# Second weight buffers for block 5, values 35 steps behind, and the end's first sums in dead keys' memory, in a one-core hybrid decoder layer

## The chip, the cores and the metric

The kernel runs on one core of a Trainium2 chip. The metric is the device time in microseconds of one execution. All numbers of the profile come from one execution taken by the hardware profiler; the times come from three other executions.

## What is computed

One decoder layer on 1024 tokens of width 1024, in float32. The input is normalized, projected to queries, keys, values and gates, and goes through two mixers side by side: eight heads of differential softmax attention, and four heads of gated linear attention (GLA). Both results are normalized by head, gated, joined, projected by `w_out`, normalized and added to the input. Cut to what the change touches, the reference is:

```python
h = rms_norm(x, pre_g)
z = jnp.einsum('bsd,de->bse', h, w_in)
qa, ka, va, ga, qb, kb, vb, gb, gk_low = split_columns(z)
# per head, two maps m = 0, 1 of width 64, causal:
s = jnp.einsum('bqhmd,bkhmd->bhmqk', qb, k)
p = jax.nn.softmax(jnp.where(mask, s, -jnp.inf), axis=-1)
w = p[:, :, 0] - lam * p[:, :, 1]
oa = jnp.einsum('bhqk,bkhv->bqhv', w, v)
oa = rms_norm(oa, subln_g) * (1.0 - lam_init)
oa = oa.reshape(B, S, DA_WIDTH) * jax.nn.silu(ga)
# ob: the GLA heads, normalized and gated
y = jnp.einsum('bse,ed->bsd', jnp.concatenate([oa, ob], axis=-1), w_out)
out = x + rms_norm(y, post_g)
```

## The kernel before

[...] The kernel has three stages.

**Projections and GLA.** Until about 634 us TensorE multiplies the normalized input by `w_in` with a Strassen-like scheme, and the four GLA heads run between. Queries, keys, values and gates of the attention heads go to DRAM (`q_d`, `k_d`, `v_d`, `g_d`), the GLA half of the mixed activations to `mixe`, and the split `w_out` to `wo_d`. This stage isn't changed.

**Attention.** Three generators yield pieces of work with a cost, and `merge` puts them in one order: it always takes a piece of the stream whose clock stands lowest. The first, `all_scores`, runs over 8 heads and in each over the query blocks 7 to 0 of 128 rows. A block and map gives one or two matmul pairs into a PSUM bank (`sc`, three banks in turn); a score takes the keys (`k`) and the same with the high and low parts swapped (`ks`). DVE moves the bank to `p0` or `p1` with the running minimum (L1037), ACT takes the exponential (L1047), POOL scales map 1 (L1053), and DVE joins both maps (L1056). What results is the weight tile `p0_{qb}`; blocks 6 and 7 have two buffers of it, blocks 0 to 5 one. The second stream, `all_values`, runs 34 units behind: `turn` transposes a weight tile (`wtr`), ACT and DVE split it (L1095, L1096), and `weigh` multiplies by the values (`po`). `attn_norm` then normalizes and gates a half head: two matmuls `ms`, the gate loaded from `g_d` (L1118), a multiplication on POOL (L1140), and a store to `mixd` (L1141). The third stream, `out_early`, multiplies what is ready by `w_out`: the GLA half of all eight row blocks, then heads 0 to 3 (`ypart`, banks `Y`). Its sums go through `yst` (two buffers, L1246) to `y_d`, the second time added by POOL's DMA (L1304).

TensorE's order is just the order in which the program is written, so `merge` decides it. The orders of the other engines and of the DMA queue on SP come from a scheduler, which places an instruction as soon as its inputs and buffers allow in its own timeline.

**The end.** When thirteen of the fourteen stores of heads 0 to 6 have been placed, `mix_pair` loads heads 4 to 6 of two row blocks (`m_raw`, L1210; split in L1331 and L1332). The sums so far are loaded from `y_d` into `yp`, a tile of the same two `yst` buffers (L1312, L1323, L1338), and ACT copies them into a PSUM bank (`seed`, L1365), so that the last matmuls (`yps`) add to them. `ENDS` is the order of the row blocks, 4 5 6 7 0 1 2 3. Then `finish` takes each block through the last norm, with `post_g` loaded in L1392 and negated on POOL in L1394.

Loads of keys and queries: `load_qk` takes one of six tags of the pool `kp` (`q0`, `q1`, `k0`, `k1`, `ks0`, `ks1`: query or key, lower or upper half of the sequence). Odd heads have their lower keys in another pool. The next head's upper half is asked for when block 4 has been placed, as only blocks 7 to 4 read it.

Of the kernel before, what the change touches and what calls it, by code (L numbers as in the profile page):

```python
# [8 lines left out]
F32 = mybir.dt.float32  # L9
# [5 lines left out]
P = 128  # L15
# [16 lines left out]
def hymba_kernel(  # L32
# [23 lines left out]
    def fp(t):  # L56
        return t.bitcast(F32)
# [810 lines left out]
    def load_qk(h, n, half):  # L868

        if h % 2 and half == 0 and n != "q":  # L870
            t = smps[0].tile([P, 2, 512], F32R, tag=f"{n}0", name=f"{n}0")
        else:
            t = kp.tile([P, 2, 512], F32R, tag=f"{n}{half}", name=f"{n}{half}")
        for m in range(2):
            d = qk_d["q" if n == "q" else "k"][h][m, :, :, cols(half)]
            if n != "ks":
                sp.dma_start(fp(t[:, m]), d.rearrange("t p s -> (t p) s"))
            else:
                for i in range(2):
                    sp.dma_start(fp(t[64 * i : 64 * i + 64, m]), d[1 - i])  # L880
        qk[h, n, half] = t

    qk, smps = {}, []


    go(order.index((12, 5)) - made[0])
# [98 lines left out]
    def load_v(h):  # L985
        v = [smp.tile([P, NT, P], F32R, tag="v", name=f"v{t}", bufs=4) for t in range(2)]
        for t in range(2):
            ins = sp.dma_start(fp(v[t]), v_d[h][t])
            if h == 0:
                tc.keep_in_program_order(ins)  # L990
        return v
# [16 lines left out]
    def scores(h, qb):  # L1008

        n = (qb + 1) * P  # L1010
        qc = slice(qb % 4 * P, qb % 4 * P + P)
        st = const.tile([P, 6], F32, tag="stt", name="stt", bufs=4)
        p0 = pp.tile([P, n], F32, tag=f"p0_{qb}", name="p0", bufs=1 + (qb > 5))
        p1 = smp.tile([P, S], F32, tag="p1", name="p1", bufs=2)
        for m, p in enumerate((p0, p1)):
            q = qk[h, "q", qb // 4][:, m, qc]
            parts = parts_of(n)
            if h == DA_HEADS - 1 and (qb, m) in ((1, 1), (0, 0), (0, 1)):

                parts = [(0, 512)]  # L1020
            for i, (a, b) in enumerate(parts):
                sc = sc_bank("sc", [P, 512])
                for j, name in enumerate(("k", "ks")):
                    for half in range(2):
                        lo, hi = max(a, half * 512), min(b, half * 512 + 512)
                        if lo < hi:
                            mm(
                                sc[:, lo - a : hi - a], q,
                                qk[h, name, half][:, m, lo - half * 512 : hi - half * 512],
                                start=(j == 0), stop=(j == 1),  # L1030
                            )
                e = min(b, n)
                last = i == len(parts) - 1

                behind = tc.issue_after(lowest[0]) if (h, qb) == (0, NT - 2) else nullcontext()
                with behind:
                    ins = dve.tensor_tensor_reduce(  # L1037
                        p[:, a:e], sc[:, : e - a],
                        maskt[:, NZ + P - (e - a) :] if last else maskt[:, : e - a],
                        1.0, 3e38 if i == 0 else st[:, 4 + m : 5 + m], ALU.add, ALU.min,  # L1040
                        st[:, m : m + 1] if last else st[:, 4 + m : 5 + m],
                    )
                if (h, qb) == (0, NT - 1):
                    lowest[:] = [ins.ins]
                c = 0.08 + (e - a) / 512 * 0.56
                if last:
                    act.activation(  # L1047
                        p[:, :n], p[:, :n], AF.Exp, bias=st[:, m : m + 1], scale=-1.0,
                        accum_out=st[:, 2 + m : 3 + m],
                    )  # L1050
                if last and m:
                    dve.reciprocal(st[:, 4:6], st[:, 2:4])  # L1052
                    pool.tensor_scalar(  # L1053
                        p1[:, :n], p1[:, :n], st[:, 5:6], lam, ALU.mult, ALU.mult
                    )
                    dve.scalar_tensor_tensor(  # L1056
                        p0[:, :n], p0[:, :n], st[:, 4:5], p1[:, :n], ALU.mult, ALU.subtract
                    )
                    w[h, qb] = p0
                    c += 0.25 + n / 1024 * 1.4  # L1060
                yield c
# [3 lines left out]
    def all_scores():  # L1065
        for h in range(DA_HEADS):
            for qb in range(NT - 1, -1, -1):
                if qb in (3, 5) and h:
                    yield lambda h=h, half=qb // 4: (h - 1, half) in used
                yield from scores(h, qb)  # L1070
                if qb == 4 and h + 1 < DA_HEADS:
                    for n in ("q", "k", "ks"):
                        load_qk(h + 1, n, 1)
                    for n in ("k", "ks"):
                        load_qk(h + 1, n, 0)
            if h + 1 < DA_HEADS:
                load_qk(h + 1, "q", 0)
        scored.append(True)
        opened.update(dict.fromkeys(SC))
# [33 lines left out]
    def attn_norm(h, half, o):  # L1113
        if h < DA_HEADS - 1:
            gate = smp.tile([P, 512], F32, tag="gate", name="gate", bufs=2)
        else:
            gate = kp.tile([P, 512], F32, tag=("q1", "k1")[half], name="gate")
        sp.dma_start(gate, g_d[h][:, cols(half)])  # L1118
        sq = smp.tile([P, 512], F32, tag="r", name="sq", bufs=1)
        act.activation(sq, o, AF.Square)  # L1120
        hl = smp.tile([P, 2, 512], F32R, tag="sq_hl", name="sq_hl", bufs=1)
        act.copy(hl[:, 0], sq)
        dve.tensor_tensor(hl[:, 1], sq, fp(hl[:, 0]), ALU.subtract)
        if h == DA_HEADS - 1:

            dve.scalar_tensor_tensor(gate, o, sub_g, gate, ALU.mult, ALU.mult)
        yield 0.0
        yield 0.0
        n_tr[0] += 1
        ms = bank(TR[n_tr[0] % 2], [P, 512], "ms")  # L1130
        for i in range(2):
            mm(ms, ones, hl[:, i], start=(i == 0), stop=(i == 1))
        if h == DA_HEADS - 1 and not half:
            opened[TR[n_tr[0] % 2]] = None
        r = smp.tile([P, 512], F32, tag="r", name="r", bufs=1)
        act.activation(r, ms, AF.Ln, bias=eps_t, scale=1.0 / P)
        act.activation(r, r, AF.Exp, scale=-0.5)
        if h < DA_HEADS - 1:
            dve.scalar_tensor_tensor(r, o, sub_g, r, ALU.mult, ALU.mult)
            pool.tensor_tensor(gate, r, gate, ALU.mult)  # L1140
            sp.dma_start(mixd[h * P : (h + 1) * P, cols(half)], gate)  # L1141
            stored.append(h)
        else:
            dve.tensor_tensor(gate, gate, r, ALU.mult)
            last_mix[half] = gate
        yield 0.0

    def all_values():
# [17 lines left out]
        for i, (h, half, kts) in enumerate(units):  # L1166
# [10 lines left out]
                yield 0.4  # L1177
                norm_step()
            if kts == (0,):
                o = smp.tile([P, 512], F32, tag="o", name="o", bufs=3)  # L1180
                po = bank(PO, [P, 512], "po")
            weigh(po, half, kts, vs[h], turned[h, half, kts])
            norm_step()
# [65 lines left out]
    def out_early():  # L1249
# [57 lines left out]
        for n, st in enumerate(ENDS[:2]):  # L1307
            if n:
                yield lambda: scored
            for dh in range(2):  # L1310
                yp = smp.tile([P, 512], F32, tag="yst", name="yp", bufs=2)
                sp.dma_start(yp, yd[st][dh])  # L1312
                seed(st, dh, (Y, SC)[n][dh], yp)
            yield 0.7
        for st in ENDS[:2]:
            for dh in range(2):
# [2 lines left out]
                    yield 0.69  # L1319
            if st == ENDS[0]:  # L1320
                mix_pair(2)
                yp = smp.tile([P, 512], F32, tag="yst", name="yp", bufs=2)
                sp.dma_start(yp, yd[ENDS[2]][0])  # L1323
                seed(ENDS[2], 0, SC[2], yp)

    def mix_pair(n):

# [6 lines left out]

    def early_ends():

        yp = smp.tile([P, 512], F32, tag="yst", name="yp", bufs=2)
        sp.dma_start(yp, yd[ENDS[2]][1])  # L1338
        for e in range(4, 7):
            last_times(ENDS[2], 0, parts_d[ENDS[2]], e)  # L1340
        for st in ENDS[:2]:
            last_part(st, parts_d[st])
            for dh in range(2):
                last_times(st, dh, parts_d[st], 7)
        seed(ENDS[2], 1, PO, yp)
        for st in ENDS[2:4]:
            last_part(st, parts_d[st])

# [18 lines left out]
    def last_times(st, dh, part, e):  # L1367
# [6 lines left out]
            )  # L1374

    T = 8 * 36.0
    LAG = 34.0
    s_cost = sum(
        2 * sum(0.08 + (min(b, n) - a) / 512 * 0.56 for a, b in parts_of(n)) + 0.25 + n / 1024 * 1.4
        for n in range(P, S + 1, P)  # L1380
# [1 line left out]
    merge(  # L1382
        [0.0, T, DA_HEADS * s_cost, all_scores()],
        [LAG, T + LAG, DA_HEADS * 10.0, all_values()],
        [-6.0, T + LAG, 16.0 + 14 * 5.52 + 16 * 2.76 + 11.8, out_early()],
    )


    smp_cm.__exit__(None, None, None)
    fin = ctx.enter_context(tc.tile_pool(name="fin", bufs=3, reuse_waits="tile"))  # L1390
    post_g = fin.tile([P, D], F32, name="post_g", bufs=1)
    sp.dma_start(post_g, post_norm_g[0:1, :].to_broadcast([P, D]))  # L1392

    pool.tensor_scalar(post_g, post_g, -1.0, None, ALU.mult)  # L1394
# [118 lines left out]
```

## Time and profile before

| | us |
|---|---|
| three runs: median | 999.5 |
| lowest and highest | 996.18, 999.75 |
| the profiled execution | 1000.02 |
| its span, first to last instruction | 998.3 |
| projections and GLA, to the first `ypart` | 633.9 |
| attention, to the first `yps` | 300.2 |
| from the first `yps` to the last matmul | 56.5 |
| after the last matmul | 7.7 |

The profile names a group by source line, engine, operation and tile. TensorE's matmuls all have line 117 and its transposes line 120, so their tiles tell them apart: `sc` for scores, `wtr` for transposed weights, `po` for values, `ypart` and `yps` for the output projection. A wait is written as the instruction that waits, its line, and what ended the wait; idle time of an engine stands in brackets in the timeline. "SPq" is the DMA queue on SP, and its times are those of issuing, not of the transfer.

### The profile page before, as it was taken

What the parts mean: (1) busy time and instruction counts of PE and PEld (TensorE: products, weight loads), DVE (VectorE), ACT (ScalarE), POOL (GpSimd) and SP (SyncE); (2) the same over time, 40 slices, a digit from 0 to 9 for tenths busy, and PEclk for the clock granted to TensorE, in tenths of its full rate; (3) what the DMA queues carried; (4) which work ended last, traced back from release to release, by engine and by line L of the source; (5) the groups of instructions that cost most, each with busy time, mean ns of one, the idle gap of its engine ahead of it and who ended that gap; (6) DMA issues with size and microseconds to landing.
All of it is one profiled execution on the core that took longest, in us unless ns stands there. A gap on an engine that the chain in (4) does not pass through costs nothing.

```text
span 998.3 us, 15795 instructions
## 1 busy us (share of the span) xinstructions
PE 966.6 (97%) x5354; PEld 835.4 (84%) x5354; DVE 728.3 (73%) x1436; ACT 591.6 (59%) x1148; POOL 133.1 (13%) x143
## 2 busy tenths in 40 slices
PE   6999999999999999999999999989999999999896
PEld 5998988888889998998888888768888888888775
DVE  6986697789757487568778684667777788787455
ACT  7642464586466446345457674356676677687573
POOL 5200000000000001000000000011322233443122
PEclk9999999999999999999999999999999999999899
DMA  9443366747766678877987768895675679984567
GB/s 356 129 120 101 111 166 211 235 153 228 262 219 193 216 232 274 263 244 239 294 248 259 246 190 302 272 369 152 212 231 170 212 267 299 336 214 97 158 190 158
DMA packets 152593, 220.45 MB, mean 221 GB/s; under 512 B 17104, under 2 KB 83664, under 8 KB 152416
## 3 DMA queue, kind: packets, MB, share of 16 engines
q1 hardware_dynamic: 148480, 212.10, 65.9%
q0 software_dynamic: 4032, 7.34, 4.6%
q8 instruction: 42, 0.69, 0.3%
q14 instruction: 39, 0.32, 0.1%
HBM read 133.93 MB, written 88.60 MB: 223 GB/s over the span
## 4 chain that ended last, share of the span: by engine, by line
PE 83%; DMA 8%; DVE 3%; ACT 3%; SPq 1%; issue 1%; POOL 0%; DVEq 0%; ACTq 0%; POOLq 0%
PE x L117 20%; PE z L117 13%; PE y L117 13%; PE ypart L117 12%; PE sc L117 6%; PE po L117 5%; PE yps L117 4%; PE wtr L120 3%; PE gpo L117 2%; DMA wo_d<-wo_raw 2%; DMA wo_raw<-in_w_out_dram 1%; PE kv L117 1%; DMA v_d<-c 1%; PE gkl_ps L117 1%; DMA m_lo<-mixe 1%
## 5 line engine op out<-in xcount | busy, mean ns | idle before, releaser
L315 ACT CAST w<-w_raw 128x512 fp32r<-128x512 f32 (+1 forms) x164 | 112.5, 688 | 98.3 <-PE y L117 46.6
L316 DVE TENSOR_TENSOR w<-w_raw,w 128x512 fp32r<-128x512 f32 (+1 forms) x164 | 126.7, 774 | 48.9 <-ACT w L315 43.1
L1047 ACT ACTIVATE p<-p,stt 128x896 f32<-128x896 f32 (+7 forms) x128 | 99.4, 777 | 48.8 <-DVE stt L1037 48.1
L427 ACT COPY s<-x 128x512 f32<-128x512 f32 x84 | 49.0, 583 | 89.5 <-PE x L117 89.3
L1037 DVE CUSTOM_DVE_ANT_0 p<-sc,maskt 128x512 f32<-128x512 f32 (+3 forms) x128 | 74.7, 586 | 31.2 <-PE sc L117 30.1
L1053 POOL TENSOR_SCALAR p<-p,stt,lam 128x1024 f32<-128x1024 f32 (+3 forms) x64 | 54.7, 855 | 261.0 <-DVE stt L1052 252.1
L296 DVE TENSOR_TENSOR w_raw<-w_raw 128x512 f32<-128x512 f32 (+1 forms) x96 | 75.6, 787 | 17.0 <-DMA w_raw<-in_w_in_dram 15.6
L117 PE MATMUL z<-s_hi,w 128*128 128x512 f32 x320 | 80.2, 393 | 0.0
L117 PE MATMUL y<-h_hi,w 128*128 128x512 f32 x320 | 80.1, 392 | 0.0
L117 PE MATMUL x<-s_hi,w 128*128 128x512 f32 x320 | 80.0, 392 | 0.0
L117 PE MATMUL ypart<-wo_hi,m_hi 128*128 128x512 f32 x192 | 78.5, 409 | 0.1
L784 POOL TENSOR_SCALAR_AFFINE_SELECT gan<-gan 128x512 f32<-128x512 f32 x8 | 10.8, 1346 | 492.5 <-ACT gan L783 492.5
L117 PE MATMUL ypart<-wo_hi,m_lo 128*128 128x512 f32 x192 | 75.4, 393 | 0.0
L117 PE MATMUL ypart<-wo_lo,m_hi 128*128 128x512 f32 x192 | 75.4, 393 | 0.0
L117 PE MATMUL sc<-k,q 128*128 128x512 f32 (+1 forms) x192 | 70.3, 371 | 4.8 <-DMA q<-q_d 2.7
L117 PEld LDWEIGHTS x<-s_hi,w 128*128 128x128 f32 x320 | 59.4, 188 | 12.0
L117 PEld LDWEIGHTS y<-h_hi,w 128*128 128x128 f32 x320 | 59.3, 188 | 11.8
L117 PEld LDWEIGHTS z<-s_hi,w 128*128 128x128 f32 x320 | 59.1, 188 | 11.7
L117 PE MATMUL sc<-ks,q 128*128 128x512 f32 (+1 forms) x192 | 66.4, 348 | 1.2 <-DMA ks<-k_d 1.2
L1096 DVE TENSOR_TENSOR wt_lo<-wtr,wt_hi 128x512 fp32r<-128x512 f32 (+1 forms) x80 | 50.5, 633 | 14.8 <-ACT wt_hi L1095 14.4
L1095 ACT CAST wt_hi<-wtr 128x512 fp32r<-128x512 f32 (+1 forms) x80 | 42.9, 538 | 27.7 <-PE wtr L120 27.4
L1056 DVE SCALAR_TENSOR_TENSOR p<-p,stt,p 128x1024 f32<-128x1024 f32 (+3 forms) x64 | 53.1, 829 | 8.0 <-POOL p L1053 7.9
(224 smaller groups left out, 2242.3 us busy)
## 6 DMA issues: line engine op xcount, KB each, us to landing
w_raw<-in_w_in_dram SPq DMA_DIRECT2D x56, 512.0 KB, 4.7
wo_raw<-in_w_out_dram SPq DMA_DIRECT2D x32, 256.0 KB, 3.3
wo_d<-wo_hi SPq DMA_DIRECT2D x32, 256.0 KB, 3.3
wo_d<-wo_raw SPq DMA_DIRECT2D x32, 256.0 KB, 3.7
q<-q_d SPq DMA_DIRECT2D x32, 256.0 KB, 5.0
k<-k_d SPq DMA_DIRECT2D x32, 256.0 KB, 6.0
ks<-k_d SPq DMA_DIRECT2D x64, 128.0 KB, 6.0
wo_hi<-wo_d SPq DMA_DIRECT2D x16, 512.0 KB, 7.0
```

The source lines that it names most:

```text
L117: tc.keep_in_program_order(pe.matmul(*a, **k))
L120: tc.keep_in_program_order(pe.transpose(dst, src, ident))
L296: dve.tensor_tensor(dst, a, b, ALU.subtract)
L315: act.copy(w[0], src)
L316: dve.tensor_tensor(w[1], src, fp(w[0]), ALU.subtract)
L427: act.copy(b[k], ps)
L1037: ins = dve.tensor_tensor_reduce(p[:, a:e], sc[:, : e - a], maskt[:, NZ + P - (e - a) :] if last else maskt[:, : e - a], 1.0, 3e38 if i == ...
L1047: act.activation(p[:, :n], p[:, :n], AF.Exp, bias=st[:, m : m + 1], scale=-1.0, accum_out=st[:, 2 + m : 3 + m],)
L1053: pool.tensor_scalar(p1[:, :n], p1[:, :n], st[:, 5:6], lam, ALU.mult, ALU.mult)
L1056: dve.scalar_tensor_tensor(p0[:, :n], p0[:, :n], st[:, 4:5], p1[:, :n], ALU.mult, ALU.subtract)
L1095: act.copy(hi[:, :n], pt[:, :n])
L1096: dve.tensor_tensor(lo[:, :n], pt[:, :n], fp(hi[:, :n]), ALU.subtract)
```

## The change

Seven edits, all in the attention stage and the end:

- Block 5's weight tile gets two buffers, as blocks 6 and 7 have. The scores of a head then wait for the transposes of the head before at block 4 in place of block 5.
- The values run 35 units behind the scores in place of 34, and the third stream is paced over 20 more units.
- The loads of values and of gates are issued behind the queries and keys that were asked for last (`issue_after` orders them in the queue).
- The sums so far of the first three row blocks come to tiles of their own in the memory of keys and queries that no head reads any more (`k0`, `ks0`, `q0`), both halves at once.
- `post_g` goes to the memory of `ks1`.
- The tile `o` has two buffers in place of three.
- `early_ends` no longer loads sums itself.

```diff
@@ load_qk
             if n != "ks":
-                sp.dma_start(fp(t[:, m]), d.rearrange("t p s -> (t p) s"))
+                ins = sp.dma_start(fp(t[:, m]), d.rearrange("t p s -> (t p) s"))
             else:
                 for i in range(2):
-                    sp.dma_start(fp(t[64 * i : 64 * i + 64, m]), d[1 - i])
+                    ins = sp.dma_start(fp(t[64 * i : 64 * i + 64, m]), d[1 - i])
+        qk_load[:] = [ins.ins]
         qk[h, n, half] = t
@@ load_v
-            ins = sp.dma_start(fp(v[t]), v_d[h][t])
+            with tc.issue_after(qk_load[0]) if h else nullcontext():
+                ins = sp.dma_start(fp(v[t]), v_d[h][t])
@@ scores
-        p0 = pp.tile([P, n], F32, tag=f"p0_{qb}", name="p0", bufs=1 + (qb > 5))
+        p0 = pp.tile([P, n], F32, tag=f"p0_{qb}", name="p0", bufs=1 + (qb > 4))
@@ all_scores
-                if qb in (3, 5) and h:
+                if qb in (3, 4) and h:
                     yield lambda h=h, half=qb // 4: (h - 1, half) in used
@@ attn_norm
-        sp.dma_start(gate, g_d[h][:, cols(half)])
+        with tc.issue_after(qk_load[0]):
+            sp.dma_start(gate, g_d[h][:, cols(half)])
@@ all_values
-                o = smp.tile([P, 512], F32, tag="o", name="o", bufs=3)
+                o = smp.tile([P, 512], F32, tag="o", name="o", bufs=2)
@@ out_early
             for dh in range(2):
-                yp = smp.tile([P, 512], F32, tag="yst", name="yp", bufs=2)
-                sp.dma_start(yp, yd[st][dh])
-                seed(st, dh, (Y, SC)[n][dh], yp)
+                seed(st, dh, (Y, SC)[n][dh], sums_of(n)[:, dh])
...
                 mix_pair(2)
-                yp = smp.tile([P, 512], F32, tag="yst", name="yp", bufs=2)
-                sp.dma_start(yp, yd[ENDS[2]][0])
-                seed(ENDS[2], 0, SC[2], yp)
+                seed(ENDS[2], 0, SC[2], sums_of(2)[:, 0])
+
+    sums_so_far = {}
+
+    def sums_of(n):
+        if n not in sums_so_far:
+            yp = sums_so_far[n] = kp.tile([P, 2, 512], F32, tag=("k0", "ks0", "q0")[n], name="yp")
+            for dh in range(2):
+                sp.dma_start(yp[:, dh], yd[ENDS[n]][dh])
+        return sums_so_far[n]
@@ early_ends
-        yp = smp.tile([P, 512], F32, tag="yst", name="yp", bufs=2)
-        sp.dma_start(yp, yd[ENDS[2]][1])
...
-        seed(ENDS[2], 1, PO, yp)
+        seed(ENDS[2], 1, PO, sums_of(2)[:, 1])
@@
-    LAG = 34.0
+    LAG = 35.0
...
-        [-6.0, T + LAG, 16.0 + 14 * 5.52 + 16 * 2.76 + 11.8, out_early()],
+        [-6.0, T + LAG + 20, 16.0 + 14 * 5.52 + 16 * 2.76 + 11.8, out_early()],
...
-    post_g = fin.tile([P, D], F32, name="post_g", bufs=1)
+    post_g = kp.tile([P, D], F32, tag="ks1", name="post_g")
```

Three places show what the scheduler and `merge` make of it. The first is the DMA queue on SP where head 0's scores run and head 1's loads are issued. `v_7050`, `v_7051` and, after, other numbers are the values of head 1; `k_6672`, `q_6669` and `ks_6675` are the upper halves of head 1's keys, queries and swapped keys. A row waits for the lane (`DMAHW0` to `DMAHW7`) that it takes over from the copy eight rows ahead. Before:

```order
L988 DMA v_7050<-v_d 128x1024 [waits DMAHW0_49]
L988 DMA v_7051<-v_d 128x1024 [waits DMAHW1_49]
L1118 DMA gate<-g_d 128x512 [waits DMAHW2_49]
L1118 DMA gate<-g_d 128x512 [waits DMAHW3_49]
L877 DMA k_6672<-k_d 128x512 [waits DMAHW4_49,PE_49]
L877 DMA q_6669<-q_d 128x512 [waits DMAHW5_49,PE_49]
L877 DMA q_6669<-q_d 128x512 [waits DMAHW6_49]
L877 DMA k_6672<-k_d 128x512 [waits DMAHW7_49]
L880 DMA ks_6675<-k_d 64x512 [waits DMAHW0_49]
L880 DMA ks_6675<-k_d 64x512 [waits DMAHW1_49]
L880 DMA ks_6675<-k_d 64x512 [waits DMAHW2_49]
L880 DMA ks_6675<-k_d 64x512 [waits DMAHW3_49]
```

The same place of the queue after the change; the four rows ahead of it are the same in both, the swapped lower keys of head 1:

```order
L877 DMA k_6672<-k_d 128x512 [waits DMAHW0_49,PE_49]
L877 DMA q_6669<-q_d 128x512 [waits DMAHW1_49,PE_49]
L877 DMA q_6669<-q_d 128x512 [waits DMAHW2_49]
L877 DMA k_6672<-k_d 128x512 [waits DMAHW3_49]
L880 DMA ks_6675<-k_d 64x512 [waits DMAHW4_49]
L880 DMA ks_6675<-k_d 64x512 [waits DMAHW5_49]
L880 DMA ks_6675<-k_d 64x512 [waits DMAHW6_49]
L880 DMA ks_6675<-k_d 64x512 [waits DMAHW7_49]
```

The values of head 1 and two gates have moved behind the keys and queries of head 1, and each of these takes the lane of another copy than before: the first of `k_6672` and of `q_6669` those of `m_hi` and `m_lo`, the four of `ks_6675` those of the four swapped lower keys.

The second place is TensorE where the last `ypart` triple stands, near the end of the last head; `p_` tiles are that head's weights. Before:

```order
L117 MATMUL ypart<-wo_hi,m_hi 128x512
L117 MATMUL ypart<-wo_hi,m_lo 128x512
L117 MATMUL ypart<-wo_lo,m_hi 128x512
L120 MATMUL wtr<-ident,p_9701 128x128
L120 MATMUL wtr<-ident,p_9648 128x128
L120 MATMUL wtr<-ident,p_9563 128x128
L120 MATMUL wtr<-ident,p_9478 128x128
L117 MATMUL po<-wt_hi,v_9748 128x512
L117 MATMUL po<-wt_hi,v_9749 128x512
L117 MATMUL po<-wt_lo,v_9748 128x512
```

After, the last `ypart` triple stands here:

```order
L117 MATMUL ypart<-wo_hi,m_hi 128x512
L117 MATMUL ypart<-wo_hi,m_lo 128x512
L117 MATMUL ypart<-wo_lo,m_hi 128x512
L117 MATMUL po<-wt_hi,v_9706 128x512
L117 MATMUL po<-wt_hi,v_9707 128x512
L117 MATMUL po<-wt_lo,v_9706 128x512
L120 MATMUL wtr<-ident,p_9753 128x128
L120 MATMUL wtr<-ident,p_9722 128x128 x2
L117 MATMUL yps<-wo_hi,m_hi 128x512
```

Before, seven of the last head's ten groups of transposes came after the last `ypart` triple; the `yps` of blocks 4 and 5 then ran between the values. After, `ypart` lasts to the last head's last group of transposes, and two triples of `yps` stand between the last values.

The third place is POOL in the last head's scores: its scalings of map 1 from block 6 on, the stores that add to `y_d`, and `post_g`. Before, `post_g` stood behind all of them, after the last gate; after:

```order
L1056 TENSOR_SCALAR p_9589<-p_9589,stt,lam 128x768
L1308 DMA y_d<-yst 128x512
L1056 TENSOR_SCALAR p_9649<-p_9649,stt,lam 128x640
L1403 TENSOR_SCALAR post_g<-post_g 128x1024
L1308 DMA y_d<-yst 128x512
L1056 TENSOR_SCALAR p_9723<-p_9723,stt,lam 128x512
```

`post_g` has moved ahead of one store and of the scalings of the last head's blocks 3 to 0, which POOL takes in this order.

More of the change, by code (lines that the diff above doesn't have):

```diff
@@ L876, in load_qk @@
             if n != "ks":
-                sp.dma_start(fp(t[:, m]), d.rearrange("t p s -> (t p) s"))
+                ins = sp.dma_start(fp(t[:, m]), d.rearrange("t p s -> (t p) s"))
             else:
                 for i in range(2):
-                    sp.dma_start(fp(t[64 * i : 64 * i + 64, m]), d[1 - i])
+                    ins = sp.dma_start(fp(t[64 * i : 64 * i + 64, m]), d[1 - i])
+        qk_load[:] = [ins.ins]
         qk[h, n, half] = t
-    qk, smps = {}, []
+    qk, smps, qk_load = {}, [], []
     go(order.index((12, 5)) - made[0])
```

## The prediction

> **What bounds the kernel now.** I read first the sums of busy time, then TensorE's waits, then a table of windows over the part that the change touches. TensorE is busy for 966.6 us of the 998.3 us span, so a change that leaves its matmuls as they are can win only where it waits or runs slowly.
>
> ```profile
> span 998.3 us, 15795 instructions
> PE 966.6 (97%) x5354; PEld 835.4 (84%) x5354; DVE 728.3 (73%) x1436; ACT 591.6 (59%) x1148; POOL 133.1 (13%) x143
> ```
>
> ```profile
> PE xT L120 <- DVE x L482: 8.8, 4, 7.4
> PE yps L117 <- ACT yps L1365: 3.2, 1, 3.2
> PE sc L117 <- DMA q<-q_d: 2.7, 1, 2.7
> PE sc L117 <- DVE stt L1037: 2.1, 3, 1.2
> PE sc L117 <- DMA ks<-k_d: 1.2, 1, 1.2
> ```
>
> The first wait belongs to the first 25 us, which the change doesn't touch. The other four lie behind 633.9 us, where attention begins; the table of windows cuts that part at them (columns: the window, its length, busy time and instructions of PE, PEld, DVE, ACT, POOL, granted clock, DMA share, GB/s).
>
> ```profile
> 633.91:664.66 30.75, 25.80 (x120) 20.18 (x119) 21.54 (x66) 16.02 (x37) 6.57 (x8) 1.00 0.92 302
> 668.20:930.90 262.70, 262.70 (x1392) 223.04 (x1390) 202.03 (x554) 184.60 (x403) 80.42 (x84) 1.00 0.72 222
> 930.90:934.08 3.18, 0.01 (x2) 0.01 (x1) 3.05 (x3) 3.12 (x7) 2.05 (x2) 0.87 0.55 94
> 934.08:940.74 6.66, 6.66 (x18) 5.31 (x19) 2.76 (x5) 1.30 (x3) 0.11 (x1) 0.55 0.69 188
> 940.74:959.37 18.63, 17.93 (x89) 14.18 (x87) 6.24 (x12) 9.61 (x20) 3.03 (x1) 1.00 0.49 160
> 990.60:998.30 7.70, 0.00 (x0) 0.00 (x0) 2.51 (x6) 1.14 (x4) 0.00 (x0) 0.77 0.18 69
> ```
>
> So the 262.7 us from 668.2 to 930.9 hold no idle time of TensorE at all. What can be won is the entry (633.9 to 668.2), the gap of 3.17 us at 930.9, and the stretch behind it, in which the clock stood at 0.55. The 7.7 us after the last matmul are the last block's norm and store, which the change leaves alone.
>
> **The entry: loads behind q and k.** The first two scores of head 1 wait:
>
> ```profile
> 664.66 0.47 PE L117 MATMUL sc<-k,q 128*128 128x512 f32 x1 [2.74 <-DMA q<-q_d]
> 667.89 0.47 PE L117 MATMUL sc<-ks,q 128*128 128x512 f32 x1 [1.17 <-DMA ks<-k_d]
> ```
>
> The chain of waits names what held those loads, and the timeline of the SP queue when each was issued:
>
> ```profile
> 649.87 6.30 DMA m_lo<-mixe
> 656.18 5.88 DMA v<-v_d
> 662.08 5.68 DMA ks<-k_d
> ```
>
> ```profile
> 654.93 1.58 SPq L988 DMA_DIRECT2D v<-v_d  x2
> 656.78 1.28 SPq L1118 DMA_DIRECT2D gate<-g_d  x2
> 658.28 0.32 SPq L877 DMA_DIRECT2D k<-k_d  x1
> 658.79 0.79 SPq L877 DMA_DIRECT2D q<-q_d  x2
> 660.86 2.94 SPq L880 DMA_DIRECT2D ks<-k_d  x4
> ```
>
> A row of the queue waits for the copy eight rows ahead of it (the lanes in the rows shown with the change). Before, the second ks copy (its first two fill the half that is asked for first) stood eight rows behind the second values copy, which landed at 662.06; so it went out at 662.08. After, values and gates stand behind, and the four ks copies stand eight rows behind the four ks copies of the other half. Those had landed by 658.28 to 659.65, since k, q, q and k went out then and waited for just these lanes. So the second ks copy can go out at about 658.8. With the landing time of the row above (5.68 us) it is there at 664.5. I take 4.5 us as the other end, as 1.5 MB of values and gates no longer run beside it: 663.3. That is 3.4 to 4.6 us before the 667.89 of the trace. Not all of it is won, since less work lies ahead of that matmul now: 60 ypart matmuls in place of 66 and 8 transposes in place of 12, by the order. At 0.23 us for a matmul and 0.09 for a transpose (spacing in the tail rows below) that is 1.7 us of work that is then still to do. **Gain 1.7 to 2.9 us, I take 2.3.** The q copy follows the same way: its first row waits for m_lo, which landed at 656.17, not for ks behind gates (658.79). Bounds: if bandwidth and not the lanes sets the landing, ks comes at 667.9 as before and the 1.7 us are lost; if both waits vanish, they and the short stalls around them give 4.6.
>
> The three waits for DVE before that (2.1 us) I leave as they are. The sixth score's eviction moves ahead of the multiply-subtract that sat waiting for POOL (below, 1.42 us), which helps one wait; but the fourth block's scores come 1.4 us sooner, and the same evictions then meet them.
>
> ```profile
> 643.83 1.29 DVE L1056 SCALAR_TENSOR_TENSOR p<-p,stt,p 128x1024 f32<-128x1024 f32 x1 [1.42 <-POOL p L1053]
> ```
>
> **The end: sums in dead keys' memory, projection spread to the end.** The wait at 930.9 names ACT's copy of the first sums into PSUM (L1365). The chain of waits shows what made ACT late:
>
> ```profile
> 921.91 1.30 POOL gate L1140
> ...
> 925.67 4.53 DMA m_raw<-mixd
> ...
> 932.56 0.97 ACT wt_hi L1095 x2
> 933.53 0.50 ACT yps L1365
> 934.08 1.65 PE yps L117 x3
> ```
>
> From the gate of head 6 to the second load of m_raw it takes 8.3 us (921.91 to 925.67 + 4.53); ACT stands in order behind it, and the split weights of the last transposes and the seed behind ACT. The sums themselves came just as late: they sit in the same two buffers as the projection's evictions, and the loads went out at 929.96 and after. The change takes both away. The loads of sums need only the keys and queries of heads 6 and 7 to be read, and the sums were stored long before. And the projection (`ypart`) is paced 20 units longer, so the order now has work where the gap was. ACT's first cast of m_raw stands there behind the eviction of the ninth triple of `ypart` from the end, and between head 6's `ms` and that triple's end stand eleven `ypart` triples, twenty-one `po`, four groups of four transposes, four scores and two `ms`: 15.8 us of TensorE. The gate comes 4.3 us behind `ms`:
>
> ```profile
> 917.60 0.62 PE L117 MATMUL ms<-sq_hl,ones 128*128 128x512 f32 x2
> 929.18 0.60 PE L120 MATMUL wtr<-ident,p 128*128 128x128 f32 x4
> 929.53 0.70 PE L117 MATMUL po<-wt_hi,v 128*128 128x512 f32 x2
> 936.80 0.63 PE L117 MATMUL yps<-wo_hi,m_hi 128*128 128x512 f32 x1
> 937.23 0.63 PE L117 MATMUL yps<-wo_hi,m_lo 128*128 128x512 f32 x1
> 948.63 0.39 PE L117 MATMUL yps<-wo_hi,m_hi 128*128 128x512 f32 x1
> 948.86 0.39 PE L117 MATMUL yps<-wo_hi,m_lo 128*128 128x512 f32 x1
> ```
>
> That leaves 11.5 us from gate to cast against the 8.3 needed, 3.2 to spare. So the gap of **3.17 us goes**. Behind it lie 18 matmuls in 6.66 us, fifteen full ones and three transposes. A full one goes each 0.43 us there (936.80 to 937.23) and each 0.23 later (948.63 to 948.86), a transpose each 0.09 (four from 929.18 to 929.53). Fifteen at 0.23 and three at 0.09 make 3.7 us, so the slow clock cost **3.0 us**, and without the gap it goes too.
>
> The granted clock fell to 0.87 in this gap of 3.17 us and to 0.55 behind it, and stayed 1.00 through the gap of 2.74 us at 664.66. [...] The rows, with the dip in the gap and right behind it, speak for the gap, and I go by them.
>
> From 940.74 to 959.37 TensorE idles 0.7 us (18.63 less 17.93), waiting for the last head's casts; after the change twelve more triples of `yps` lie behind the last values and cover that. But the last split of weights now stands in ACT behind an eviction, two casts and a seed (0.5 to 0.6 us each), with 2.4 us of TensorE work to hide it; I put 0.6 us on that. The two cancel.
>
> **What else moves, at nothing.** post_g's load and its multiplication on POOL move ahead of head 7's last four scalings:
>
> ```profile
> L1394 POOL TENSOR_SCALAR post_g<-post_g x1: 3028/3028/3028, 947.4 to 947.4; 128x1024 f32<-128x1024 f32 x1
> DMA to landing us min/median/max: 4.7/4.7/4.7
> ```
>
> The load goes out when head 7's upper keys are read, behind two gates (0.4 us each). The multiplication so ends 0.9 + 0.5 + 4.7 + 3.0 = 9.1 us after that read began. By the order, the next row on POOL, a store of the projection, would be due 8.7 us after it: the eviction that it stores follows the exponentials of head 7's fourth block. That is half a us late, and 3 us are to spare (above) before TensorE meets it. Later values and gates cost nothing: by the order a value tile is loaded more than 20 us of TensorE work ahead of its use, and a gate some 5, with 3 to 5 us to land. The second buffer of block 5 and the third `o` taken away touch no wait of TensorE in the rows above. The 35 steps put scores earlier against values (7.1 us from a head's block 4 to its first transpose, 6.4 before, by the order), so no new wait there. Between ends: none of this can help in a stretch that has no idle time, and 2.1 us in each head, as head 0 pays now, is the price if the new order makes evictions late.
>
> **The sum.** The profiled execution took 1000.0 us (span 998.3 and 1.7 around it), 0.5 above the median of the three runs. 1000.0 - 3.2 - 3.0 - 2.3 = **991.5 us**; that the median lies 0.5 lower is within the error.
>
> **Rivals.**
> - *The entry gives nothing*: bandwidth sets the landing. For it: the DMA share there is 0.92. 993.8 to 995.5. Chance 0.13.
> - *The end's gap stays*, because m_raw's chain is later than I count (post_g holds POOL, gate and store slip by over 3.2 us): only the entry is won, 997.7. Chance 0.10.
> - *The dip is not the gap's*: gap gone, slow clock stays: 994.5. Chance 0.05. [...]
> - *Slower*: scores stand closer in some heads (three banks are reused within 1.7 us of work at the closest, 2.3 before), and the eviction waits of head 0 (2.1 us) come in the seven other heads: 14.7 - 8.5, so 1006. Against it: DVE is busy 202 of 262.7 us there and never held TensorE. It decides from 8.5 / 7 = 1.2 us a head. Chance 0.10.
> - *My forecast*: 0.62.
>
> Counting each case by where it falls against 994.5 and 1004.5 (0.5% of 999.5, about what a measurement of this kernel can tell from no change): faster 0.70, same 0.21, slower 0.09. The range goes from 987.5 (both entry waits and the stalls around them gone, 2.3 more; the tail's 0.6 hidden after all; half of the 2.1 us of evictions gone) to 997.5 (the gap at the end stays); the slow rival is left out.
>
> **What will show it.** Right: no wait of `yps` for ACT's seed over 0.5 us and a clock of 1.00 from 900 us to the last matmul; ks of head 1 issued by 659 and its wait ended by 664.5; no idle time of TensorE between. Wrong: a wait of `sc` for `stt` in heads 1 to 7, of `ms` or `po` for DVE behind post_g, or of `yps` for m_hi at the end; any one of over 3 us brings the slow clock with it.

## The result, and the profile after

| | before | after |
|---|---|---|
| median of six executions each, us | 998.45 | 990.35 |
| lowest and highest | 996.18, 999.85 | 987.71, 991.54 |
| ratio, 95% interval | | 0.9917, 0.9898 to 0.9936 |
| the profiled execution | 1000.02 | 991.11 |
| its span | 998.3 | 989.4 |

The changed kernel takes 8.1 us less; 991.5 was forecast. The page of the profile after, its span and sums of busy time:

```profile
span 989.4 us, 15789 instructions
PE 964.9 (98%) x5354; PEld 835.2 (84%) x5354; DVE 727.8 (74%) x1436; ACT 591.0 (60%) x1148; POOL 133.3 (13%) x143
```

What TensorE waited for from 630 to 990 us (the answer to the lines of before on `yps`, `q`, `ks` and `stt`):

```profile
PE sc L117 <- DVE stt L1040: 1.9, 3, 1.0
PE ms L117 <- DVE sq_hl L1127: 1.2, 2, 0.8
PE sc L117 <- DMA ks<-k_d: 0.7, 1, 0.7
PE wtr L120 <- DVE wt_lo L1099: 0.2, 1, 0.2
```

The waits for the sums and for q are gone, that for ks has shrunk, and 1.4 us of short waits of `ms` and `wtr` for DVE's splits are new (operands are split into a high part and a low remainder, `hi` and `lo` in the rows; a product of two split ones is three matmuls). The waits for `stt` stand elsewhere: 1.3 us in head 0, where it was 2.1 before, and 0.66 us at head 1's first score, in the place of the wait for q. The windows of after, from the first `ypart` to the last matmul (columns as in the prediction):

```profile
635.53:661.45 25.92, 23.81 (x111) 18.63 (x109) 19.64 (x60) 14.45 (x32) 5.28 (x6) 1.00 0.93 292
661.45:667.50 6.05, 5.31 (x26) 4.22 (x27) 4.89 (x15) 3.29 (x8) 1.32 (x3) 1.00 1.05 364
667.50:932.90 265.40, 264.06 (x1402) 223.37 (x1401) 205.85 (x555) 187.02 (x407) 82.62 (x86) 1.00 0.75 230
932.90:982.71 49.81, 49.80 (x229) 41.14 (x227) 26.91 (x69) 31.60 (x87) 11.35 (x13) 1.00 0.76 169
```

Two windows of before complete those that the prediction shows:

```profile
664.66:668.20 3.54, 2.36 (x12) 1.79 (x13) 1.56 (x4) 0.58 (x1) 0.00 (x0) 1.00 1.07 347
930.90:990.52 59.62, 55.74 (x242) 44.68 (x241) 32.12 (x75) 35.70 (x93) 15.74 (x15) 0.94 0.72 181
```

From these rows: from its first `ypart` to its last matmul, before takes 356.6 us (346.6 busy, 10.0 idle) and after 347.2 (343.0 busy, 4.2 idle). So 5.8 us come from idle time and 3.6 from busy time, which is the slow clock, as the matmuls are the same. Behind the last matmul another 1.1 us go (7.8 to 6.7). That makes 10.5 us in this pair of traces; the stage began 1.6 us later in the execution of after, and 8.9 us separate the two profiled times.

### The profile page after: what moved, and what is told of

It is laid out like the page before. It is cut to its first block, busy times and chain, and to the rows that moved or that the text cites. A ratio compares the mean times of both kernels' runs of the same rounds, so it can differ in the third digit from the quotient of the medians.

```text
span 989.4 us, 15789 instructions
## 1 busy us (share of the span) xinstructions
PE 964.9 (98%) x5354; PEld 835.2 (84%) x5354; DVE 727.8 (74%) x1436; ACT 591.0 (60%) x1148; POOL 133.3 (13%) x143
## 4 chain that ended last, share of the span: by engine, by line
PE 91%; DMA 3%; DVE 2%; ACT 2%; issue 1%; POOL 1%; SPq 0%; DVEq 0%; POOLq 0%; ACTq 0%
PE x L117 23%; PE y L117 16%; PE z L117 15%; PE ypart L117 11%; PE sc L117 6%; PE po L117 5%; PE yps L117 4%; PE wtr L120 3%; PE gpo L117 3%; PE kv L117 1%; DMA ks<-k_d 1%; DMA v_d<-c 1%; PE gkl_ps L117 1%; PE pa L117 1%; PE ms L117 1%
## 5 line engine op out<-in xcount | busy, mean ns | idle before, releaser
L1050 ACT ACTIVATE p<-p,stt 128x384 f32<-128x384 f32 (+7 forms) x128 | 99.3, 777 | 53.6 <-DVE stt L1040 53.0
L1040 DVE CUSTOM_DVE_ANT_0 p<-sc,maskt 128x512 f32<-128x512 f32 (+3 forms) x128 | 73.4, 583 | 12.3 <-PE sc L117 11.5
L784 POOL TENSOR_SCALAR_AFFINE_SELECT gan<-gan 128x512 f32<-128x512 f32 x8 | 13.0, 1624 | 492.4 <-ACT gan L783 492.4
L1059 DVE SCALAR_TENSOR_TENSOR p<-p,stt,p 128x1024 f32<-128x1024 f32 (+3 forms) x64 | 53.3, 836 | 11.4 <-POOL p L1056 11.2
```

Of the source, the lines that this page charges most:

```text
L1040: ins = dve.tensor_tensor_reduce(p[:, a:e], sc[:, : e - a], maskt[:, NZ + P - (e - a) :] if last else maskt[:, : e - a], 1.0, 3e38 if i == ...
L1050: act.activation(p[:, :n], p[:, :n], AF.Exp, bias=st[:, m : m + 1], scale=-1.0, accum_out=st[:, 2 + m : 3 + m],)
L1059: dve.scalar_tensor_tensor(p0[:, :n], p0[:, :n], st[:, 4:5], p1[:, :n], ALU.mult, ALU.subtract)
```

## The experiments

Each ran beside the kernel before on the same chip, whose median was 998.6 to 999.1 there. The changed kernel stands at 0.9917 and, the second time, at 0.9915. Losses against the changed kernel are differences of these ratios, times 999 us; a ratio is known to 1.2 to 2.6 us either way. "Stage" is the time from the first `ypart` to the end of the last matmul in the kernel's own trace (before 356.6, after 347.2), which is one execution.

| kernel | median, us (executions) | ratio to before, 95% interval | stage, us |
|---|---|---|---|
| loads_ahead | 994.95 (7) | 0.9956, 0.9941 to 0.9972 | 350.5 |
| sums_back | 996.90 (11) | 0.9985, 0.9973 to 0.9997 | 352.2 |
| pace_short | 996.07 (12) | 0.9969, 0.9955 to 0.9983 | 352.7 |
| fill_gap | 999.07 (12) | 1.0001, 0.9988 to 1.0014 | 353.7 |
| loads_only | 997.42 (12) | 0.9982, 0.9970 to 0.9994 | 353.0 |
| one_buffer5 | 994.50 (6) | 0.9952, 0.9935 to 0.9969 | 352.8 |
| one_buffer5_again | 993.11 (9) | 0.9946, 0.9927 to 0.9965 | 350.0 |
| lag_34 | 990.99 (6) | 0.9926, 0.9911 to 0.9942 | 349.1 |
| early_9 | 996.58 (12) | 0.9979, 0.9966 to 0.9991 | 353.3 |
| after_again | 990.49 (6) | 0.9915, 0.9890 to 0.9939 | 346.1 |
| v_late | 989.75 (6) | 0.9911, 0.9885 to 0.9937 | 346.8 |

### The entry: loads_ahead, loads_only, v_late

`loads_ahead` is the changed kernel with

```diff
-            with tc.issue_after(qk_load[0]) if h else nullcontext():
+            with nullcontext():
                 ins = sp.dma_start(fp(v[t]), v_d[h][t])
...
-        with tc.issue_after(qk_load[0]):
+        with nullcontext():
             sp.dma_start(gate, g_d[h][:, cols(half)])
```

> The changed kernel with the values and gates no longer held behind the queries and keys; TensorE's order is the same row for row. My theory (the lanes of the SP queue): the second ks copy of head 1 again waits for the second values copy, so ks is issued some 3.4 us later than the 658.7 of the changed kernel and the score pair that needs it waits 3 to 5 us instead of 0.7; 993 to 995 us against 990.35. Rival (bandwidth sets the landing): ks lands when it does now, 990 to 991 us.

It was 994.95 us, by the ratios about 3.9 above the changed kernel, so the entry's edit pays. But the wait came in another place than I expected. In its timeline of TensorE and in its windows:

```profile
662.30 0.47 PE L117 MATMUL sc<-k,q 128*128 128x512 f32 x1 [3.37 <-DMA q<-q_d]
```

```profile
660.16:663.58 3.42, 1.27 (x6) 1.04 (x7) 1.26 (x4) 0.08 (x1) 0.55 (x1) 1.00 1.06 386
663.58:667.00 3.42, 3.42 (x12) 2.55 (x11) 2.11 (x9) 1.46 (x4) 0.00 (x0) 0.50 1.05 377
```

The queue on SP, first `loads_ahead`, then the changed kernel:

```profile
656.47 0.85 SPq L877 DMA_DIRECT2D q<-q_d  x2
658.44 2.95 SPq L880 DMA_DIRECT2D ks<-k_d  x4
```

```profile
656.14 1.16 SPq L877 DMA_DIRECT2D q<-q_d  x2
658.68 2.37 SPq L880 DMA_DIRECT2D ks<-k_d  x4
```

Counted from the first `ypart` (633.66 and 635.53) q goes out 2.2 us later and ks 1.6 later. Counted on the queue itself, from the first load of head 1's lower keys, the three traces without the edit agree (`loads_ahead`, `fill_gap` and before: 8.4 to 9.0 us to q, 10.4 to 11.1 to ks), and so do the nine with it that keep head 0's values in front (5.6 to 6.5, and 7.6 to 9.6). In `loads_ahead` q stands behind the issuing of values and gates again, and the ks copies wait for the lanes that were named (the queue's own waits in `loads_ahead` between 655 and 662 us); after, the chain of waits has the second ks copy behind the landing of a copy of the other half:

```profile
SPq L880 <- DMA v<-v_d: 1.4, 2, 0.8
```

```profile
651.90 7.25 DMA ks<-k_d
659.17 4.98 DMA ks<-k_d
```

The wait is for q, 3.37 us in place of 0.66 (for DVE) and 0.74 (for ks): 2.0 us more idle. Behind it the clock stood at 0.50 for 3.42 us, which costs another 1.7. Idle and clock together make 3.7 of the 3.9.

`loads_only` adds the same lines to the kernel before, and nothing else:

> The kernel before with the loads of values and gates held behind queries and keys, and nothing else of the change; TensorE's order is that of the kernel before row for row. My theory (the lanes): the ks copies of head 1 go out some 3.4 us earlier, the two waits of 3.9 us fall to 0.5 us or so, and the gap at the end stays: 995 to 996 us against 998.8, unless a lowered clock covers the same time. Rival (this edit pays only together with the new order): 998 to 999 us.

Both waits for DMA vanish from its trace. Yet 997.42 is only 1.6 us below the kernel before on that chip, where 3 were expected. The traces offer a reason. This one has a stretch of half clock from 650.5 to 653.9, behind the waits for `stt` in head 0. So has `fill_gap`, whose entry is that of the kernel before, with this wait at its end in place of 2.74 and 1.17:

```profile
667.92 0.47 PE L117 MATMUL sc<-ks,q 128*128 128x512 f32 x1 [0.76 <-DMA ks<-k_d]
```

```profile
651.10:654.52 3.42, 3.42 (x11) 2.74 (x10) 2.26 (x7) 2.05 (x4) 0.00 (x0) 0.50 0.98 380
```

In `fill_gap` the pair that needs ks starts at 667.92, in the trace of before at 667.89, though TensorE came to it some 3.4 us later: 1.7 by the half clock, 1.7 because the stage began at 635.63 and not at 633.91. The waits were shorter by about as much: DMA set the time there, and the slow clock ahead of it cost nothing. With the loads early it counted. Behind the first `ypart` the pair stands at 34.0 us in before, 32.3 in `fill_gap` and 31.1 in `loads_only`; against `fill_gap`, which has the old entry and the same half clock, the edit gains 1.2 us. That is how removing waits of 3.9 us can bring 1.6. It is read from single traces and not shown for the timed executions, and the stage of `loads_only` (352.95) is 3.7 us shorter than that of before (356.61).

`v_late` is the changed kernel with head 0's values behind head 1's upper q, k and ks as well:

```diff
-    v_first = load_v(0)
+    v_first = []
...
                         load_qk(h + 1, n, 1)
+                    if h == 0:
+                        v_first.extend(load_v(0))
```

> The changed kernel with the values of head 0 (1 MB) loaded behind the upper q, k and ks of head 1 too; TensorE's order is the same. If what is left of the entry's waits for DMA (0.7 us in the first trace of the changed kernel, 2.3 with one buffer for block 5) comes from these bytes going first, q and ks land 1 to 3 us earlier and no wait for them is left: 988 to 990 us. If the values then come late, po of head 0 waits at about 31 us behind the start of the stage: 991 to 993 us.

It was 989.75 us, ratio 0.9911 against 0.9915: no difference that this measurement can tell. Waits for q and ks are gone, and `po` waits 0.4 us for the values. What was left of the entry's DMA waits was worth less than can be measured here.

### The end: sums_back, pace_short, fill_gap, lag_34

`sums_back` is the changed kernel with the sums in `yst` again; TensorE's order stays:

```diff
-                seed(st, dh, (Y, SC)[n][dh], sums_of(n)[:, dh])
+                yp = smp.tile([P, 512], F32, tag="yst", name="yp", bufs=2)
+                sp.dma_start(yp, yd[st][dh])
+                seed(st, dh, (Y, SC)[n][dh], yp)
```

and the same at the other two places of the diff.

> The changed kernel with the sums so far loaded into the two yst buffers again, the pace of 20 units more kept; TensorE's order is the same row for row. Theory 1 (the sums' own buffers are needed): the last two evictions of the projection leave at 930.7 and 935.8 and their stores take some 4 us, so the sums can be loaded only from about 936, and the first yps, at 936.2 now, waits 3 us, the second half's about 3 more, with a lower clock behind it: 994 to 1000 us. Theory 2 (the longer pace alone removed the gap): at most 0.5 us of wait, 990 to 991 us.

By the ratios 6.9 us are lost. The timeline has the loads where the stores of the last evictions let them go, and the wait behind them (rows of SP's queue and of TensorE):

```profile
935.48 7.22 SPq L1316 DMA_DIRECT2D yp<-y_d  x4
...
938.71 0.50 PE L117 MATMUL yps<-wo_hi,m_hi 128*128 128x512 f32 x1 [2.75 <-ACT yps L1380]
```

```profile
936.54:939.95 3.41, 1.24 (x5) 1.05 (x6) 1.30 (x3) 1.15 (x3) 0.51 (x1) 0.99 0.93 151
939.95:943.36 3.41, 3.41 (x13) 3.06 (x12) 0.41 (x1) 2.12 (x4) 0.00 (x0) 0.51 0.54 153
```

2.75 idle, 1.7 by the clock and 1.0 behind the last matmul make 5.5 of the 6.9. The pace alone did not remove the gap. (From the last matmul to the end it is 7.7 to 7.8 us in the four kernels with the sums in `yst`, before among them, and 6.6 to 6.7 in all others. Up to the issue of the last store it is 2.7 us in before and after alike; then the queue on SP waits 2.6 to 2.7 us for that store in the four, and 1.5 in after, `pace_short`, `lag_34` and `v_late`. What ties this to the sums, the profile doesn't say.)

`pace_short` is the changed kernel with one number put back:

```diff
-        [-6.0, T + LAG + 20, ...
+        [-6.0, T + LAG, ...
```

> The changed kernel with the third stream paced as before (no 20 units more); the sums keep their own memory. Theory 1 (the chain gate, store, load, cast of m_raw sets the end): with the projection done earlier nothing is left to lie beside the chain, so yps waits 2 to 4 us again and the clock falls behind it: 993 to 997 us. Theory 2 (only the sums in yst made the gap): no wait of yps above 0.5 us, 990 to 991 us.

By the ratios 5.3 us are lost, as by theory 1, but `yps` waits only 0.7 us, for `m_hi` and `m_lo` as it did before. The chain of m_raw holds ACT, and ACT holds the transposes and the values (timeline, rows of ACT and PE):

```profile
928.57 0.51 ACT L1342 CAST m_hi<-m_raw 128x384 fp32r<-128x384 f32 x1 [3.40 <-DMA m_raw<-mixd]
...
929.72 0.66 PE L120 MATMUL wtr<-ident,p 128*128 128x128 f32 x4 [1.03 <-ACT r L1140]
932.17 0.74 PE L117 MATMUL po<-wt_hi,v 128*128 128x512 f32 x2 [1.09 <-ACT wt_hi L1098]
933.79 0.51 PE L117 MATMUL po<-wt_lo,v 128*128 128x512 f32 x1 [0.89 <-DVE wt_lo L1099]
```

```profile
930.90:934.32 3.42, 1.45 (x5) 0.78 (x5) 3.23 (x5) 3.42 (x8) 2.32 (x2) 1.00 0.20 77
934.32:937.74 3.42, 3.42 (x11) 2.67 (x11) 1.25 (x2) 1.25 (x3) 0.00 (x0) 0.50 0.96 158
```

So either of two things is enough to hold TensorE at this place: ACT in order behind m_raw, and the sums behind the evictions. Undoing either edit brings back about as much as the gap and the slow clock had cost together (6.2). Neither was made alone in the kernel before.

`fill_gap` is the kernel before with dead work in the gap; their sum is overwritten and no output depends on it:

```diff
+        opened[SC[2]] = bank(SC[2], [P, 512], "yps")
+        for _ in range(14):
+            mm(opened[SC[2]], ones, wo[4][0][:, :512], start=True, stop=True)
         for st in ENDS[:2]:
```

> The kernel before, with 14 full matmuls whose result nobody reads put right ahead of the first yps, so that TensorE works through its gap of 3.17 us. Theory 1 (the idle gap brings the slow clock): the clock stays at 1.00 behind the gap and the 18 matmuls there take 3.7 instead of 6.7 us: 995 to 996 us against 998.4. [...]

The clock is 1.00 through the filled gap and behind it, where before has 0.87 and 0.55, so the idle time did bring the dip. But the time is that of the kernel before (windows, and two rows of TensorE's timeline):

```profile
930.61:933.91 3.30, 3.30 (x18) 2.54 (x16) 3.17 (x3) 3.24 (x7) 2.05 (x2) 1.00 0.59 109
933.91:938.62 4.71, 4.33 (x20) 2.94 (x19) 2.23 (x4) 0.59 (x1) 0.14 (x1) 1.00 0.73 192
```

```profile
934.70 0.62 PE L117 MATMUL po<-wt_hi,v 128*128 128x512 f32 x2
935.60 0.50 PE L117 MATMUL po<-wt_lo,v 128*128 128x512 f32 x1 [0.27 <-DVE wt_lo L1096]
```

The 18 matmuls take 4.71 us, not 3.7: at full clock they come to the halves of split weights, and at 938.62 to ACT's copy of the next sums, before ACT and DVE are done. From 933.91 to the matmul at which both kernels wait for m_hi (953.45; 934.08 to 954.70 before) it is 19.5 us against 20.6. So of 3.0 us of slow clock only 1.1 could be won in that order, which the interval of the ratio (1.3 us either way) does not exclude; the rest was hiding waits for the splits and the sums. In the changed kernel, with `ypart` between them, there are none in the trace, and the 3.0 are won in full.

`lag_34` is the changed kernel with `LAG = 34.0`.

> The changed kernel with the values 34 units behind the scores in place of 35. My theory (the end hangs on the 20 units of pace and on the sums, not on this unit): 989.5 to 991.5 us against 990.35. Rival (the unit is what gives the m_raw chain its margin): a wait at the end of 2 us or more and a lowered clock behind it, 993 to 996 us.

990.99 us and 0.9926 against 0.9915 to 0.9917: no difference shown. Its trace has one wait of `ms` of 1.7 us near the end and a half-clock stretch behind it, so a cost of some 1 us is not excluded.

### The rest: one_buffer5 twice, early_9, after_again

`one_buffer5` is the changed kernel with block 5 as before:

```diff
-        p0 = pp.tile([P, n], F32, tag=f"p0_{qb}", name="p0", bufs=1 + (qb > 4))
+        p0 = pp.tile([P, n], F32, tag=f"p0_{qb}", name="p0", bufs=1 + (qb > 5))
...
-                if qb in (3, 4) and h:
+                if qb in (3, 5) and h:
```

> The changed kernel with one buffer again for the weights of block 5, the scores waiting for the head before at block 5 again; the lag of 35 and the pace are kept. My theory (this edit touches no wait of TensorE): 989.5 to 991.5 us, within half a per cent of the changed kernel's 990.35. Rival (the second buffer is what lets the scores and the projection spread without a wait): waits of sc or wtr between 667 and 932 us of 2 us or more in all, 992.5 us or more.

> The changed kernel with one buffer for the weights of block 5, a second time. If its 2.08 us wait before head 1's first score belonged to that one execution (q landed about 1 us later against the start of the stage), that wait is 1 us or less now and what stays is the waits in heads 1 to 7, some 3 us against 1.3: 992 to 994 us. If the edit makes the entry late, the wait stands there again: 994 to 995 us.

994.50 and 993.11 us: by the ratios 3.5 and 3.1 us above the changed kernel, by the medians 4.2 and 2.6. Each interval alone overlaps that of the changed kernel a little, but the two runs agree. My theory is refuted. The wait of 2.1 us at the entry in the first trace was that execution's; in the second, TensorE's waits from 667 to 990 us are

```profile
PE sc L117 <- DVE stt L1040: 1.0, 2, 0.6
PE ms L117 <- DVE sq_hl L1127: 0.8, 2, 0.5
PE wtr L120 <- DVE wt_lo L1099: 0.6, 1, 0.6
```

which is 1.0 us more than the changed kernel's (1.4). At the entry it waits 0.9 us for ks, where `after_again` has no such wait and the first trace of the changed kernel 0.7. The stage is 3.9 us longer than in `after_again`, with no half clock in either. 2.1 of it is idle time; 1.7 us more of busy time at a clock of 1.00 no view explains, and I leave that open. Two of the waits are scores waiting for an eviction in the later heads, which the changed kernel has in neither trace. Likely the scores, held at block 5, stand closer together there; that was not followed.

`early_9` begins the third stream at -9.0 in place of -6.0.

> The changed kernel with the third stream begun at -9 in place of -6, so that more of the projection stands between head 0's scores. If the waits of sc for DVE that are left in head 0 (1.9 us) come from scores that stand too close, they shrink by 1 to 1.9 us: 988.5 to 989.5 us against 990.35. If the evictions are late for another cause, or the projection's own tiles are not there yet, it is 990 to 992 us.

It is 6 us slower, which neither case foresaw. The three waits for `stt` became one of 2.0 us at 651.6, and near the end `po` waits 4.0 us for ACT (sums of waits):

```profile
PE po L117 <- ACT o L1189: 4.0, 1, 4.0
PE sc L117 <- DVE stt L1040: 2.0, 1, 2.0
```

Half clock follows both (0.50 in the window from 652 to 654 us, and from 917.9 to 924.7). The chain of waits leads the second one back to `post_g`: its load takes 7.2 us to land, its multiplication holds POOL to 912.5, the scalings of map 1 come behind it, DVE waits for them and ACT for DVE (rows of the chain and of DVE's timeline):

```profile
902.20 7.17 DMA post_g<-in_post_norm_g_dram
...
914.23 1.67 DVE L1059 SCALAR_TENSOR_TENSOR p<-p,stt,p 128x512 f32<-128x512 f32 x2 [3.42 <-POOL p L1056]
```

`after_again` is the changed kernel itself:

> The changed kernel itself a second time, beside the next two on the same chip, for a second trace of it. Theory 1 (short idle times bring 3.3 us of half clock at places that change from one execution to the next): the waits of TensorE stay within 0.5 us of the first trace's at the same places, while the half-clock stretches lie elsewhere or are missing; 989 to 992 us. Theory 2 (the half clock of 27 to 30 us in the first trace belongs to the kernel): it stands at 27 us again.

Behind 630 us the waits stand where they stood, to 0.1 us, but that for ks (0.7) is gone. The half clock of 27 to 30 us is gone too, and one from 464.9 to 468.3, behind a wait of 2.1 us in the GLA part, has come; the first trace waits 1.6 us at that place and keeps its clock. That is theory 1; 990.49 us repeats the first 990.35.

## Why the prediction was right

**The entry.** ks went out at 658.68 and its wait ended at 664.29, both within what was forecast, and the wait for q is gone. But these are times from the span's start, and the stage began 1.6 us later than before. Against the work the ks pair stands 28.8 us behind the first `ypart`, 34.0 before, and 5.2 less 1.7 of work is a gain of 3.5 in these traces, where I took 2.3. Not all of it is the edit's: in the trace of before the whole queue was late, with head 1's lower keys asked for 16.5 us behind the first `ypart` against 13.9 to 15.2 in the twelve other traces. That the loads do it, and bandwidth doesn't undo it, `loads_ahead` showed: 3.9 us lost without. The forecast's mechanism, the lanes, is what the queue's waits and issue times show; what it left out is the half clock behind the wait.

**The waits for `stt`**: 2.1 forecast as unchanged, 1.9 measured, but only 1.3 of them in head 0.

**The end.** The gap of 3.17 us is gone, and the clock stands at 1.00 from 667.5 us to the last matmul. I had counted 11.5 us from the gate to the cast of m_raw; the trace has 11.4:

```profile
915.71 1.29 POOL L1144 TENSOR_TENSOR gate<-r,gate 128x512 f32<-128x512 f32 x1 [2.17 <-DVE r L1143]
...
927.07 0.93 ACT L1342 CAST m_hi<-m_raw 128x384 fp32r<-128x384 f32 x2
```

The cast followed an eviction at once, without a wait. `pace_short` and `sums_back` showed that both halves of the step were needed. **The slow clock**, 3.0, came as forecast: busy time fell by 3.6. It was not a gain that could be added to any order, though: in the order of before, `fill_gap` removed it and won nothing that could be measured.

**The tail.** 0.7 gone against 0.6 new was forecast; after 932.9 TensorE idles 0.01 us, so the new 0.6 did not come. Nothing was forecast behind the last matmul, where 1.1 us went; they come and go with the sums' place, for a reason that no view shows.

**post_g** was to cost nothing, with 3 us to spare. Its load took 5.9 us to land where 4.7 was counted, its multiplication ended at 911.2, and the chain that ends in the wait of `ms` for DVE of 0.39 us at 920.32 goes through it: the spare time was used up. In `lag_34` (7.3 us to land) such a chain ends in the wait of `ms` of 1.7 us, in `early_9` in that of 4.0. No run put `post_g` back, so its price is read from chains and not shown.

**At nothing** stood also the second buffer of block 5. Here the prediction was wrong: "touch no wait of TensorE in the rows above" was true of the old order, but the buffer is what keeps the new one nearly free of waits, and the two runs of `one_buffer5` show it to be worth some 3 us. The forecast sum was not harmed, since it forecast no new waits. The third `o` taken away was not tried alone.

**The rivals.** The entry gave something, and the gap went. No score waited for an eviction behind 667.5 us; the 1.3 us of idle time up to 932.9 (265.40 less 264.06) are `ms` and `wtr` waiting for DVE's splits, 0.2 a head against the 1.2 from which the slower case decides. By these the sign "no idle time of TensorE between" was missed. That the dip is not the gap's is refuted by `fill_gap`'s clock.

**The sum.** That 991.5 came within 1.2 us of 990.35 is in part luck. In the traces the entry gave 3.5 for 2.3, the part from the ks pair to the last matmul 5.9 for 6.2, and what follows it 1.1 where nothing was forecast; the stage's later start took 1.6 back.

The undone edits lose 3.9, 6.9, 5.3 and some 3 us, some 19 together, where the change wins 8.1. They are links of one order: a link missing brings back from a third to most of what the whole gained.

## What to carry to other kernels

Where one engine is busy throughout, look for what each removed wait was covering: a slow clock or late split behind it can take its place. In `fill_gap` 18 matmuls took 4.71 us at a clock of 1.00 where 3.7 were counted, and `loads_only` had half clock from 650.5 to 653.9 us. Test the parts of such a change by taking one out of the whole, not only by adding one to the old kernel, as the parts pay together. A forecast of "no effect" for a buffer has to be made in the order after, not in the rows of before.

## What the runs showed of the hardware

The half clock came in stretches of 3.4 us, alone or two in a row (`before` 933.28 to 940.10 us, `early_9` 917.9 to 924.7), and not with each wait. In the ten places where the 3.4 us ahead of it were read, TensorE had been busy for 0.91 to 1.92 us of them and idle for the other 1.5 to 2.5, from several waits together as well as from one. The second stretch of a row followed 2.62 us of busy time in `before` and 1.79 in `early_9`, themselves at half clock. One more pair, from `lag_34`, beside the three above:

```profile
915.59:919.00 3.41, 1.70 (x5) 0.86 (x5) 2.21 (x6) 3.37 (x9) 1.87 (x3) 1.00 0.80 243
919.00:922.41 3.41, 3.34 (x10) 2.87 (x11) 2.02 (x5) 1.72 (x4) 2.16 (x2) 0.50 1.06 195
```

Busy in the 3.4 us ahead were 1.27, 1.24, 1.45 and 1.70 us in these four. A gap of 2.74 us in the trace of before was followed by none (busy 0.68 of the 3.42 us up to 664.66, and the clock 1.00 in the 3.4 us behind), and a wait of 1.0 us at 26 us by one in the first trace of after and none in the second. So the waits of over 3 us, of which the prediction's last line speaks, were not needed, and no figure for what brings the slow clock follows from these traces. A stretch costs up to 1.7 us, an estimate from its 3.4 us and its clock of 0.50; in the trace of before a full matmul went each 0.43 us in it and each 0.23 at 1.00. The mean granted clock of an execution was 0.993 in the median of 67 of the kernel before, 0.995 in its one trace, and 0.997 and 0.998 in the medians of the changed kernel's two runs; so executions of before mostly held more half clock than its trace shows, and that has gone as well. That these stretches also make the scatter between executions is an estimate, which was not tested.
